# Feed-forward groups in another order, squares summed in parts, and the last shift shared between two engines

## The chip, the cores and the metric

The kernel runs on one core of one Trainium2 chip. The metric is the device time of one execution in microseconds (us). Five engines work side by side and wait for each other by semaphores: TensorE (PE, with its weight load PEld), VectorE (DVE), ScalarE (ACT), GpSimd (POOL) and SyncE (SP, which here only issues transfers). Sixteen DMA engines move data between the chip's memory (HBM) and the on-chip memory (SBUF); TensorE writes its products to PSUM.

## The reference, cut to what matters

Two decoder layers are run for a prompt of 256 tokens and a sample group of 8 sequences of 4 tokens (288 tokens together), with model width 1024. Layer 0 mixes tokens by retention, layer 1 by gated DeltaNet (GDN); each is followed by a gated feed-forward of width 2816. Ahead of each of these four parts, and once more at the end, the activations are normed and modulated by vectors that are computed from a condition (adaLN):

```python
def ada_rmsnorm(x, g, shift, scale):
    xf = x.astype(jnp.float32)
    xn = xf * lax.rsqrt(jnp.mean(xf * xf, axis=-1, keepdims=True) + EPS) * g.astype(jnp.float32)
    return (xn * (1.0 + scale[:, None, :]) + shift[:, None, :]).astype(x.dtype)

def conv_ffn(h, buf, w_up, w_dw, b_dw, w_down):
    up = jnp.einsum('btd,df->btf', h, w_up)
    gate_br, val = up[..., :D_FF], up[..., D_FF:]
    conv, new_buf = causal_dwconv(gate_br, buf, w_dw)
    act = jax.nn.silu(conv + b_dw.astype(conv.dtype)) * val
    return jnp.einsum('btf,fd->btd', act, w_down), new_buf
...
        h = ada_rmsnorm(x, p['norm_ffn'][l], sh2, sc2)
        out, buf = conv_ffn(h, s_fconv[l], p['w_ffn_up'][l], p['w_ffn_dw'][l], p['b_ffn_dw'][l], p['w_ffn_down'][l])
        x = (x.astype(jnp.float32) + g2[:, None, :] * out.astype(jnp.float32)).astype(x.dtype)
    y = ada_rmsnorm(x, p['norm_final'], shf, scf)
```

The outputs are y, the new states of both mixers and the last rows of the convolutions.

## The kernel before

Activations lie transposed: x is 8 tiles of 128 channels by 288 tokens. Weights come from HBM in blocks of 128 x 1024 (512 KB). Each block is split into a high and a low part (`whi` by ACT, line 414; `wlo` by DVE, line 415), and each product is made of three: high by high, high by low, low by high (`product`, line 533). One block serves 24 matmuls of 288 columns.

**Feed-forward** (`ffn`). The 22 tiles of the inner width are worked in groups of four, four, four, four, four and two. For each tile there is a gate product `fg` and a value product `fv`, with convolution, silu and product on ACT and DVE between them, and the result is split into `fah` and `fal`. The down product of a group (`down`) runs after the up products of the next group. `down` walks over the 8 tiles of x: a group of four tiles gives 12 matmuls for each tile of x, a group of two gives 6. After them DVE adds the gated result to x (line 698), forms the sample part `dt` (line 700), and POOL adds that (line 702). In the last group ACT also squares the new tile of x (line 595, `sq`, the first one into `ssum`) and DVE adds it to `ssum` (line 599).

**The norm** (`token_rsqrt`, `modulated`). The squares are summed over channels by products with a column of ones (`st`, line 558, 3 products of one column for each part that is summed, one for each of three stretches of 128 tokens; each is two instructions in the profile). DVE works out the reciprocal root from the 3 columns (lines 545 to 550, eleven small instructions), TensorE spreads it over the partitions (`rb`, line 564), and DVE and ACT make the modulated tiles `hh` and `hl` (lines 621 to 634). In the last feed-forward (gate 11) the squares of tiles 5, 6 and 7 are not added by DVE but kept as parts of their own, so that `st_y` is 12 products; the other places have one part and 3 products.

**The condition's products** (`adaP`, line 453) are cut into steps and put in where TensorE would wait: before `st`, between `st` and `rb`, and behind it.

**The end** (`finish`). After the last norm the result `yt` goes out in four transfers of two tiles each, from SP and ACT in turn.

Loads are issued by SP in the order of a plan (`plan_weights`) as their buffers come free. The order of the instructions on each engine is set by the framework's scheduler from the recorded program; it is read below from the built program.

Of the kernel before, what the change touches and what calls it, by code (L numbers as in the profile page):

```python
# [14 lines left out]
P = 128  # L15
# [7 lines left out]
KH, VH = 8, 16  # L23
FF = 2816
FT = FF // P
HALF_TOK = (0, 128, T - 128)
RSQRT_MAGIC = 0x5F3759DF
QUANTUM = 6
# [34 lines left out]
SAMPLE_STEPS = 3  # L63
OUT_STEPS = 1
SQ_ADD = 5
QK_STEPS = 5
ROOT_STEPS = 4
V_STEPS = 2
# [108 lines left out]
def blocks_out(w):  # L177

    out = []
    k0 = 0  # L180
    while k0 < w.shape[0]:
        n = min(4, (w.shape[0] - k0) // P)
        c = 1024 // n
        g = w[k0 : k0 + n * P].reshape(n, P, DM)
        for q in range(DM // c):
            out.append(g[:, :, q * c : (q + 1) * c].transpose(1, 0, 2).reshape(P, n * c))
        k0 += n * P
    return np.stack(out)
# [105 lines left out]
class Program:  # L294
# [12 lines left out]
    def plan_weights(self):  # L307
        A = self.A
        ada = lambda ch: [("ada", ch, k, A["wada"][ch * KT + k]) for k in range(KT)]
        wl = lambda name, i0, n: [("w", name, 0, A[name][i]) for i in range(i0, i0 + n)]  # L310

        def mix(main, extra, first=2):
            step = (len(main) - first - 1) * GROUP / max(1, len(extra))
            out, e = [], 0
            for i, m in enumerate(main):
                out.append(m)
                while e * GROUP < len(extra) and i >= first + e * step:
                    out += extra[e * GROUP : (e + 1) * GROUP]
                    e += 1
            return out + extra[e * GROUP :]  # L320


        second, step = ada(1), -(-KT // (EARLY - LATE))
        plan = [ada(0)]
        for i in range(EARLY):
            plan[0] += wl("wri", i, 1) + second[i * step : (i + 1) * step]
        ret = []
        for h in range(RH):
            ret += wl("wri", 12 * h, 12)
            if h:  # L330
                ret += wl("wro", 4 * (h - 1), 4)
        ret += wl("wro", 12, 4)
        fill = [sum((ada(ch) for ch in range(*r)), []) for r in FILL]
        plan.append(mix(ret[EARLY:], ada(2) + ada(3) + ada(4)) + fill[0])
        for l in range(2):
            f = []
            for g in range(6):
                f += wl(f"wu{l}", 8 * g, 8 if g < 5 else 4)
                if g:
                    f += wl(f"wd{l}", 4 * (g - 1), 4)  # L340
            f += wl(f"wd{l}", 20, 2)
            early = sum((ada(ch) for ch in ((range(FILL[0][1], FILL[1][0]), range(FILL[2][1], 14))[l])), [])
            plan.append(mix(f, early) + (fill[1] if l == 0 else []))
            if l == 0:
                f = wl("wba", 0, 1)
                first = {"K": 0, "V": 4, "Z": 8}
                chunk, more = F1, []
                for c, g in GDN_ORDER:
                    if c == "A":
                        more = ada(chunk)  # L350
                        chunk += 1
                        continue
                    w = wl("wgo", 4 * g, 4) if c == "D" else wl("wgi", 12 * g + first[c], 4)
                    for i, b in enumerate(w):
                        f += more[2 * i : 2 * i + 2] + [b]
                    more = []
                plan.append(f + fill[2])
        self.plan = [(*b, ph) for ph, part in enumerate(plan) for b in part]

        order, n = [], 0  # L360
        for ph, part in enumerate(plan):
            idx = list(range(n, n + len(part)))
            n += len(part)
            head = idx[:AHEAD] if ph > 1 else []
            order = order[: len(order) - (len(fill[ph - 2]) - AHEAD_AT if head else 0)] + head + (order[len(order) - (len(fill[ph - 2]) - AHEAD_AT) :] if head else []) + idx[len(head) :]
        self.order = order
        self.to_prep = [i for i, b in enumerate(self.plan) if b[0] == "w"]
        self.n_dma = self.n_prep = self.n_use = 0
        self.raw, self.split = {}, {}
        self.extra, self.held = {}, {"raw": 0}  # L370
        self.ada_todo = [i for i, b in enumerate(self.plan) if b[0] == "ada"]
# [180 lines left out]
    def token_rsqrt(self, ssum, scale, name):  # L552

        nc = self.nc
        st = self.aux(f"st_{name}")
        for i, t0 in enumerate(HALF_TOK):
            for n, s in enumerate(ssum):
                nc.tensor.matmul(st[:, i : i + 1], lhsT=s[:, t0 : t0 + P], rhs=self.ones[:, 0:1], start=(n == 0), stop=(n == len(ssum) - 1))
        r = self.tmp.tile([P, 3], F32, tag="tr", name=f"tr_{name}", bufs=2)
        self.rsqrt(r, st[:, 0:3], scale, EPS, name)  # L560
        yield from self.pause(ROOT_STEPS)
        rb = self.aux(f"rb_{name}")
        for i, c in enumerate((0, 0, P - TS)):
            nc.tensor.matmul(
                rb[:, i * P : i * P + P - c], lhsT=r[:, i : i + 1].to_broadcast([P, P]), rhs=self.ident[:, c:], start=True, stop=True
            )
        return rb[:, 0:T]
# [33 lines left out]
    def modulated(self, norm, sh, sc, name, hi, lo=None, rb=None, m0=0, m1=KT):  # L601

        nc = self.nc
        n, ms = m1 - m0, slice(m0, m1)
        am = self.tmp.tile([P, KT, 9], F32, tag="am", name=f"am_{name}", bufs=2)[:, 0:n]
        nb = self.prm("norms")[:, norm * KT + m0 : norm * KT + m1].unsqueeze(2).to_broadcast([P, n, 9])
        nc.vector.scalar_tensor_tensor(am, self.mod[:, sc * 8 + m0 : sc * 8 + m1, :], 1.0, nb, ALU.add, ALU.mult)
        shift = self.mod[:, sh * 8 + m0 : sh * 8 + m1, :]
        if rb is None:
            self.ada_due(FILLS[0])  # L610
            gen = self.token_rsqrt(self.ssum, 1.0 / DM, name)
            next(gen)

        hs = self.tmp.tile([P, T], F32, tag="t288", name=f"hs_{name}", bufs=T288)[:, : n * TS].rearrange("p (m t) -> p m t", m=n)
        by_t = lambda v: v.rearrange("p m (t b) -> p m t b", b=NB)
        by_b = lambda v: v[:, :, 1:9].unsqueeze(2).to_broadcast([P, n, TD, NB])
        nc.vector.tensor_tensor(by_t(hs), by_t(self.x[:, ms, TP:]), by_b(am), ALU.mult)
        if rb is None:
            self.ada_due(FILLS[1])
            rb = self.now(gen)  # L620
        nc.vector.tensor_tensor(hs, hs, rb[:, TP:].unsqueeze(1).to_broadcast([P, n, TS]), ALU.mult)
        if lo is None:
            nc.vector.tensor_tensor(by_t(hi[:, ms, TP:]), by_t(hs), by_b(shift), ALU.add)
        else:
            nc.vector.tensor_tensor(by_t(hs), by_t(hs), by_b(shift), ALU.add)
            nc.scalar.copy(hi[:, ms, TP:], hs)  # L626
            nc.gpsimd.tensor_tensor(lo[:, ms, TP:], hs, hi[:, ms, TP:].bitcast(F32), ALU.subtract)
        for i in range(n):
            m = m0 + i
            h = self.tmp.tile([P, T], F32, tag="t288", name=f"h_{name}", bufs=T288)[:, :TP]  # L630
            nc.vector.scalar_tensor_tensor(h, self.x[:, m, :TP], am[:, i, 0:1], rb[:, :TP], ALU.mult, ALU.mult)
            nc.scalar.activation(hi[:, m, :TP], h, AF.Identity, bias=shift[:, i, 0:1])  # L632
            if lo is not None:
                nc.vector.scalar_tensor_tensor(lo[:, m, :TP], h, shift[:, i, 0:1], hi[:, m, :TP].bitcast(F32), ALU.add, ALU.subtract)
        self.ada_due(FILLS[2])
# [50 lines left out]
    def down(self, wn, acts, kts, gate, last):  # L686
# [3 lines left out]
        for q in range(8 // per):  # L690
            w = self.weights(wn)
            for j in range(per):
# [8 lines left out]
                xv = xm[:, TP:].rearrange("p (t b) -> p t b", b=NB)  # L701
                (nc.vector if gate == 11 and last and m == KT - 1 else nc.gpsimd).tensor_tensor(xv, xv, t, ALU.add)  # L702
                if last:
                    self.squares(m, gate == 11)

    def stacked(self, out, src, which, mk):

# [200 lines left out]
    def ffn(self, l, hs, gate, after):  # L908
        nc, A = self.nc, self.A
        with ExitStack() as ctx:  # L910
# [8 lines left out]
            tail = fp.tile([P, FT, 2], F32, tag="tail", name="ftail")  # L919
            wd, bd = self.prm(f"wfd{l}"), self.prm(f"bfd{l}")  # L920
            pend = None
            for g in range(6):
                n = 4 if g < 5 else 2
                ah = ap.tile([P, 4, T], F32R, tag="ah", name=f"fah{l}{g}")
                al = ap.tile([P, 4, T], F32R, tag="al", name=f"fal{l}{g}")
                for j in range(n):
                    m = 4 * g + j
                    w = [wd[:, i * FT + m : i * FT + m + 1] for i in range(3)]
                    b = bd[:, m : m + 1]
                    pg = self.proj(hs, f"fg{l}{m}", f"wu{l}")  # L930
# [768 lines left out]
    def finish(self):  # L1699
        nc = self.nc  # L1700
        yt = self.hp.tile([P, KT, T], F32, tag="hh", name="yt")
        self.modulated(4, 12, 13, "y", yt)
        for c in range(0, KT, 2):
            (nc.sync, nc.scalar)[c // 2 % 2].dma_start(self.A["y"][:, c : c + 2], yt[:, c : c + 2])

# [22 lines left out]
```

## Time and profile before

| | |
|---|---|
| median of 3 runs | 1231.98 us (1230.52 to 1234.35) |
| profiled execution | 1235.09 us, of which the span of the profile is 1233.3 us |
| PE busy, PEld busy | 1162.4 us (94%), 1045.2 us (85%) |
| DVE, ACT, POOL busy | 877.2 us (71%), 608.4 us (49%), 326.0 us (26%) |
| chain that ended last | PE 77%, DVE 13%, ACT 3%, DMA 3%, issue 2% |
| HBM | 236.06 MB read, 31.39 MB written, 217 GB/s over the span |

The stages, in us from the span's start: start and retention to 343, the change to feed-forward 0 from 343 to 362, feed-forward 0 to 572, the change to GDN to 592, GDN to 973, the change to feed-forward 1 to 992, feed-forward 1 to 1215.5, the last norm and the output to 1233.3. "Granted clock" is the share of TensorE's full speed that it was given: 1.00 is 2.4 GHz and 0.50 is 1.2 GHz. A wait is named after the instruction that ended it.

### The profile page before, as it was taken

Reading aid. Unit: us, or ns where it says so; the run is one execution under the profiler, and the core shown is the slowest. Engines: PE = TensorE matmul, PEld = TensorE weight load, DVE = VectorE, ACT = ScalarE, POOL = GpSimd, SP = SyncE. Lnnn points to the kernel's source line nnn. Section 1 sums busy time; section 2 is a strip of 40 time slices with the busy share of each in tenths; the row PEclk is TensorE's granted clock in tenths of the full one; section 3 lists DMA queues with packets and bytes.
Section 4 is the critical chain, followed back from the end, with each engine's and each line's share of the span. In section 5 each row is a group of like instructions: output and inputs, shape, how many; then the busy total and the mean of one; then the engine's idle time right before and its main releaser. Section 6 shows DMA issues by size and latency. Waiting matters only on the chain.

```text
span 1233.3 us, 24974 instructions
## 1 busy us (share of the span) xinstructions
PE 1162.4 (94%) x9486; PEld 1045.2 (85%) x9486; DVE 877.2 (71%) x2038; ACT 608.4 (49%) x1258; POOL 326.0 (26%) x504
## 2 busy tenths in 40 slices
PE   6999999999999999999889888988899899999996
PEld 2879788797969999997777777977789699999996
DVE  3657574765766666667769888797965687878785
ACT  2444534344446445543674655745544365555542
POOL 0214142151301221233242124243222212233241
PEclk9999999999999999999989998999999899999997
DMA  9999696866689556556636652534334997878521
GB/s 350 347 335 331 224 338 230 315 239 236 226 298 400 196 161 199 171 181 243 219 84 209 218 165 61 161 129 120 126 109 130 307 358 257 258 238 264 182 76 39
DMA packets 97480, 269.08 MB, mean 218 GB/s; under 512 B 26816, under 2 KB 28832, under 8 KB 97232
## 3 DMA queue, kind: packets, MB, share of 16 engines
q1 hardware_dynamic: 87456, 234.42, 56.6%
q0 software_dynamic: 8032, 29.16, 6.3%
q10 hardware_dynamic: 1872, 3.90, 0.9%
q8 instruction: 75, 1.23, 0.4%
q14 instruction: 45, 0.37, 0.1%
HBM read 236.06 MB, written 31.39 MB: 217 GB/s over the span
## 4 chain that ended last, share of the span: by engine, by line
PE 77%; DVE 13%; ACT 3%; DMA 3%; issue 2%; POOL 1%; ACTq 0%; POOLq 0%; DVEq 0%
PE down L533 17%; PE fg L533 12%; PE fv L533 11%; PE pg L533 4%; PE pv L533 4%; PE adaP L453 4%; PE p L533 3%; PE gv L533 2%; PE gz L533 2%; DVE mp L1319 2%; DVE wlo L415 2%; PE gk L533 2%; PE pO L884 1%; PE pU L903 1%; PE pS L854 1%
## 5 line engine op out<-in xcount | busy, mean ns | idle before, releaser
L415 DVE TENSOR_TENSOR wlo<-more,whi 128x1024 fp32r<-128x1024 f32 x138 | 171.1, 1241 | 80.6 <-ACT whi L414 67.8
L414 ACT CAST whi<-more 128x1024 fp32r<-128x1024 f32 x138 | 144.4, 1048 | 139.6 <-PE down L533 53.3
L414 ACT CAST whi<-raw 128x1024 fp32r<-128x1024 f32 x123 | 128.0, 1044 | 146.3 <-PE down L533 44.1
L415 DVE TENSOR_TENSOR wlo<-raw,whi 128x1024 fp32r<-128x1024 f32 x123 | 154.2, 1256 | 60.6 <-ACT whi L414 36.5
L702 POOL TENSOR_TENSOR x<-x,dt 128x32 f32<-128x32 f32 x159 | 103.1, 649 | 138.9 <-DVE dt L700 137.2
L698 DVE SCALAR_TENSOR_TENSOR x<-down,mod,x 128x256 f32<-128x256 f32 x160 | 76.7, 479 | 52.5 <-PE down L533 51.9
L580 POOL TENSOR_TENSOR fal<-cv,fah 128x288 fp32r<-128x288 f32 x44 | 41.2, 936 | 217.3 <-ACT fah L579 186.3
L533 PE MATMUL down<-fal,whi 128*128 128x288 f32 x352 | 64.5, 295 | 0.0
L533 PE MATMUL down<-fah,whi 128*128 128x288 f32 x352 | 62.2, 294 | 0.0
L533 PE MATMUL down<-fah,wlo 128*128 128x288 f32 x352 | 62.1, 294 | 0.0
L904 DVE SCALAR_TENSOR_TENSOR S<-S,pU 128x512 f32<-128x512 f32 x64 | 42.2, 684 | 24.5 <-PE pU L903 24.4
L533 PE MATMUL fg<-hh_ffn,whi 128*128 128x288 f32 x352 | 58.4, 298 | 0.8 <-ACT hh_ffn L626 0.7
L533 PE MATMUL fv<-hh_ffn,whi 128*128 128x288 f32 x352 | 58.7, 297 | 0.0
L533 PE MATMUL fg<-hh_ffn,wlo 128*128 128x288 f32 x352 | 55.0, 296 | 0.0
L533 PE MATMUL fv<-hh_ffn,wlo 128*128 128x288 f32 x352 | 54.7, 295 | 0.0
L533 PE MATMUL fv<-hl_ffn,whi 128*128 128x288 f32 x352 | 54.2, 295 | 0.0
L533 PEld LDWEIGHTS fg<-hh_ffn,whi 128*128 128x128 f32 x352 | 50.3, 188 | 4.6 <-ACT hh_ffn L632 2.2
L533 PE MATMUL fg<-hl_ffn,whi 128*128 128x288 f32 x352 | 54.0, 295 | 0.0
L533 PEld LDWEIGHTS down<-fal,whi 128*128 128x128 f32 x352 | 52.4, 188 | 0.4 <-issue 0.4
L533 PEld LDWEIGHTS down<-fah,whi 128*128 128x128 f32 x352 | 51.9, 188 | 0.8 <-ACT whi L414 0.8
L533 PEld LDWEIGHTS fv<-hh_ffn,whi 128*128 128x128 f32 x352 | 50.3, 188 | 2.5 <-ACT ftail L934 1.2
L533 PEld LDWEIGHTS down<-fah,wlo 128*128 128x128 f32 x352 | 51.9, 188 | 0.0
(467 smaller groups left out, 2921.3 us busy)
## 6 DMA issues: line engine op xcount, KB each, us to landing
more<-in_wu SPq DMA_DIRECT2D x73, 512.0 KB, 5.2
raw<-in_wada SPq DMA_DIRECT2D x69, 512.0 KB, 4.8
raw<-in_wgi SPq DMA_DIRECT2D x48, 512.0 KB, 3.9
more<-in_wada SPq DMA_DIRECT2D x43, 512.0 KB, 6.3
more<-in_wd SPq DMA_DIRECT2D x36, 512.0 KB, 3.8
S<-in_sr SPq DMA_DIRECT2D x16, 1024.0 KB, 8.5
out_rs<-S POOLq DMA_DIRECT2D x16, 1024.0 KB, 6.9
raw<-in_wri SPq DMA_DIRECT2D x28, 512.0 KB, 4.6
```

Source lines behind the costliest of these rows:

```text
L414: nc.scalar.copy(hi[:, :c], r)
L415: nc.vector.tensor_tensor(lo[:, :c], r, hi[:, :c].bitcast(F32), ALU.subtract)
L453: nc.tensor.matmul(self.adaP[32 * g : 32 * g + 32, 0:256], lhsT=self.cs[:, k, :], rhs=rv[:, :, g, :], start=(k == 0), stop=(k == KT - 1), ...
L533: self.nc.tensor.matmul(out, lhsT=av[:, k, c0 : c0 + m], rhs=b[:, k, :], start=(k0 == 0 and i == 0), stop=(k1 == kts and i == len(seq) - 1))
L580: (nc.gpsimd if pool_lo else nc.vector).tensor_tensor(lo, src, hi.bitcast(F32), ALU.subtract)
L698: nc.vector.scalar_tensor_tensor(xm[:, :TP], p[:, :TP], g[:, 0:1], xm[:, :TP], ALU.mult, ALU.add)
L702: (nc.vector if gate == 11 and last and m == KT - 1 else nc.gpsimd).tensor_tensor(xv, xv, t, ALU.add)
L854: nc.tensor.matmul(pS, lhsT=kt[:, j, c * P : (c + 1) * P], rhs=vt[:, j, :], start=(j == 0), stop=(j == 1))
L884: nc.tensor.matmul(pO4[32 * g : 32 * g + 32, :], lhsT=qm[:, c, 4 * bb + g, :], rhs=S[bb, c][:, g, :], start=(bb == 0 and c == 0), stop=Fal ...
L903: nc.tensor.matmul(pU, lhsT=kms[g][:, c * P : (c + 1) * P], rhs=vst, start=True, stop=True)
L904: nc.vector.scalar_tensor_tensor(S[bb, c][:, g, :], S[bb, c][:, g, :], gamma4, pU, ALU.mult, ALU.add)
L1319: nc.vector.tensor_tensor(m, Ti[:, 0:k, :].rearrange("p j c -> p c j").unsqueeze(1).to_broadcast([P, w, 8, k]), X[:, 0:k, i:k].rearrange(" ...
```

## The change

1. The feed-forward's groups become two, four, four, four, four, four. The plan of loads and the layout of the down weights follow: the block pair of the two tiles comes first. The count of blocks, products and bytes is the same.
2. `squares` is called in its "end" form at all four places: three additions by DVE (tiles 5, 6 and 7) go at the end of retention, of feed-forward 0 and of GDN, and each of these norms has four parts, 12 products instead of 3. `token_rsqrt` walks over the parts outside and over the token stretches inside, so that only the last 3 products need the last tile's square.
3. In the last norm, the sample part's shift is added by POOL instead of DVE, and the prompt part of tile 2 by POOL instead of ACT.
4. The four output transfers carry tiles 0 to 3, 4 and 5, 6, and 7.

```diff
+FF_GROUPS = [(0, 2)] + [(2 + 4 * g, 4) for g in range(5)]
+POOL_TILE = 2
@@ blocks_out
-        n = min(4, (w.shape[0] - k0) // P)
+        n = 2 if (w.shape[0] - k0) // P % 4 else 4
@@ plan_weights
-            for g in range(6):
-                f += wl(f"wu{l}", 8 * g, 8 if g < 5 else 4)
+            for g, (m0, n) in enumerate(FF_GROUPS):
+                f += wl(f"wu{l}", 2 * m0, 2 * n)
                 if g:
-                    f += wl(f"wd{l}", 4 * (g - 1), 4)
-            f += wl(f"wd{l}", 20, 2)
+                    f += wl(f"wd{l}", *((0, 2) if g == 1 else (4 * g - 6, 4)))
+            f += wl(f"wd{l}", 18, 4)
@@ token_rsqrt
-        for i, t0 in enumerate(HALF_TOK):
-            for n, s in enumerate(ssum):
-                nc.tensor.matmul(st[:, i : i + 1], lhsT=s[:, t0 : t0 + P], rhs=self.ones[:, 0:1], start=(n == 0), stop=(n == len(ssum) - 1))
+        for n, s in enumerate(ssum):
+            for i, t0 in enumerate(HALF_TOK):
+                nc.tensor.matmul(
+                    st[:, i : i + 1], lhsT=s[:, t0 : t0 + P], rhs=self.ones[:, 0:1],
+                    start=(n == 0 and i == 0), stop=(n == len(ssum) - 1 and i == 2), skip_group_check=True,
+                )
@@ modulated
         if lo is None:
-            nc.vector.tensor_tensor(by_t(hi[:, ms, TP:]), by_t(hs), by_b(shift), ALU.add)
+            nc.gpsimd.tensor_tensor(by_t(hi[:, ms, TP:]), by_t(hs), by_b(shift), ALU.add)
...
-            nc.scalar.activation(hi[:, m, :TP], h, AF.Identity, bias=shift[:, i, 0:1])
+            if lo is None and i == POOL_TILE:
+                nc.gpsimd.tensor_scalar(hi[:, m, :TP], h, shift[:, i, 0:1], None, ALU.add)
+            else:
+                nc.scalar.activation(hi[:, m, :TP], h, AF.Identity, bias=shift[:, i, 0:1])
@@ down
-                    self.squares(m, gate == 11)
+                    self.squares(m, True)
@@ ffn
-            for g in range(6):
-                n = 4 if g < 5 else 2
+            for g, (m0, n) in enumerate(FF_GROUPS):
...
-                    m = 4 * g + j
+                    m = m0 + j
@@ finish
-        for c in range(0, KT, 2):
-            (nc.sync, nc.scalar)[c // 2 % 2].dma_start(self.A["y"][:, c : c + 2], yt[:, c : c + 2])
+        for i, (c, d) in enumerate(((0, 4), (4, 6), (6, 7), (7, 8))):
+            (nc.sync, nc.scalar)[i % 2].dma_start(self.A["y"][:, c:d], yt[:, c:d])
```

The order on TensorE between retention's last down product and feed-forward 0, before (`adaP` are products for the condition, `st_ffn` the sums of squares, `rb_ffn` the spread root):

```order
L453 MATMUL adaP<-raw,c 32x256 x5
L558 MATMUL st_ffn_3804<-ones,ssum 128x1 x3
L453 MATMUL adaP<-raw,c 32x256 x11
L462 MATMUL adaT<-cst,adaev 128x128 x2
L453 MATMUL adaP<-more_3786,c 32x256 x4
L564 MATMUL rb_ffn_3865<-cst,tr_ffn_3808 128x128 x2
```

and now:

```order
L455 MATMUL adaP<-raw,c 32x256 x4
L561 MATMUL st_ffn_3801<-ones,ssum 128x1 x3
L561 MATMUL st_ffn_3801<-ones,sq 128x1 x9
L455 MATMUL adaP<-raw,c 32x256 x12
L464 MATMUL adaT<-cst,adaev 128x128 x2
L455 MATMUL adaP<-more_3783,c 32x256 x4
L570 MATMUL rb_ffn_3871<-cst,tr_ffn_3814 128x128 x2
```

All twelve sums stand behind 14 instead of 15 products for the condition (the last row of these is shown), and one more product stands between them and `rb`.

The order on TensorE between feed-forward 0 and GDN, before (names as above; 32 products of `adaP` in seven rows stand ahead, the last three are shown):

```order
L453 MATMUL adaP<-more_6230,c 32x256 x4
L453 MATMUL adaP<-more_6232,c 32x256 x4
L453 MATMUL adaP<-more_6234,c 32x256 x4
L558 MATMUL st_gdn<-ones,ssum 128x1 x3
L462 MATMUL adaT<-cst,adaev 128x128 x2
L453 MATMUL adaP<-more_6274,c 32x256 x4
L453 MATMUL adaP<-more_6308,c 32x256 x4
L453 MATMUL adaP<-more_6348,c 32x256 x4
L453 MATMUL adaP<-more_6388,c 32x256
L564 MATMUL rb_gdn<-cst,tr_gdn 128x128 x2
```

and now, where the first row is the last of 20 products:

```order
L455 MATMUL adaP<-more_6248,c 32x256 x4
L561 MATMUL st_gdn<-ones,ssum 128x1 x3
L561 MATMUL st_gdn<-ones,sq 128x1 x9
L455 MATMUL adaP<-more_6250,c 32x256 x4
L455 MATMUL adaP<-more_6252,c 32x256 x4
L455 MATMUL adaP<-more_6254,c 32x256 x4
L464 MATMUL adaT<-cst,adaev 128x128 x2
L455 MATMUL adaP<-more_6294,c 32x256 x4
L455 MATMUL adaP<-more_6334,c 32x256 x4
L455 MATMUL adaP<-more_6374,c 32x256 x4
L570 MATMUL rb_gdn<-cst,tr_gdn 128x128 x2
```

The sums moved ahead of 12 products, which with the transposition `adaT` now stand between them and `rb`: 24 products there instead of 13.

The order on TensorE at the end, before:

```order
L533 MATMUL down<-fah_14525,wlo 128x288 x2
L558 MATMUL st_y<-ones,ssum 128x1
L558 MATMUL st_y<-ones,sq 128x1 x3
L558 MATMUL st_y<-ones,ssum 128x1
L558 MATMUL st_y<-ones,sq 128x1 x3
L558 MATMUL st_y<-ones,ssum 128x1
L558 MATMUL st_y<-ones,sq 128x1 x3
L564 MATMUL rb_y<-cst,tr_y 128x128 x2
```

and now:

```order
L535 MATMUL down<-fal_14290,whi 128x288 x4
L535 MATMUL down<-fah_14289,wlo 128x288 x4
L561 MATMUL st_y<-ones,ssum 128x1 x3
L561 MATMUL st_y<-ones,sq 128x1 x9
L570 MATMUL rb_y<-cst,tr_y 128x128 x2
L570 MATMUL rb_y<-cst,tr_y 128x32
```

Before, the first three of the four products of each stretch could run ahead of the last square only in the first stretch; now nine of the twelve stand ahead of the three that read it. The last down products are of a group of four.

## Rows read from the trace of the kernel before

**Rows 1.** Windows, TensorE: us, PE busy (instructions), granted clock, DMA share, GB/s.
```profile
343.00:362.00 19.00, 16.76 (x169) 1.00 0.92 344
...
973.00:992.00 19.00, 15.54 (x142) 0.82 0.95 351
...
992.00:1197.00 205.00, 205.00 (x1645) 1.00 0.70 231
...
1197.00:1215.50 18.50, 18.48 (x141) 1.00 0.12 35
```

**Rows 2.** Timeline, retention to feed-forward 0: start, us, instructions, count [idle before <-releaser].
```profile
343.80 0.94 ACT L595 ACTIVATE sq<-x 128x288 f32<-128x288 f32 x2 [1.06 <-POOL x L702]
...
344.12 0.81 PE L453 MATMUL adaP<-raw,c 128*32 128x256 f32 x8
...
345.49 0.83 PE L558 MATMUL st_ffn<-ones,ssum 128*128 128x1 f32 x6 [0.56 <-DVE ssum L599]
...
346.25 1.50 PE L453 MATMUL adaP<-raw,c 128*32 128x256 f32 x22
...
349.22 0.86 PE L564 MATMUL rb_ffn<-cst,tr_ffn 128*128 128x128 f32 x6
```

**Rows 3.** Timeline, feed-forward 0 to gated DeltaNet, TensorE.
```profile
573.34 2.34 PE L453 MATMUL adaP<-more,c 128*32 128x256 f32 x40
...
576.72 0.83 PE L558 MATMUL st_gdn<-ones,ssum 128*128 128x1 f32 x6 [1.04 <-DVE ssum L599]
...
577.75 1.92 PE L453 MATMUL adaP<-more,c 128*32 128x256 f32 x26
...
579.87 0.82 PE L564 MATMUL rb_gdn<-cst,tr_gdn 128*128 128x128 f32 x6 [0.20 <-DVE tr_gdn L550]
```

**Rows 4.** Timeline, gated DeltaNet to feed-forward 1, TensorE.
```profile
975.95 0.83 PE L558 MATMUL st_ffn<-ones,ssum 128*128 128x1 f32 x6 [0.92 <-DVE ssum L599]
...
980.42 1.08 PE L453 MATMUL adaP<-raw,c 128*32 128x256 f32 x8 [0.24 <-DMA raw<-in_wada]
...
982.53 1.33 PE L564 MATMUL rb_ffn<-cst,tr_ffn 128*128 128x128 f32 x6
```

**Rows 5.** Windows, TensorE, around the two falls of the granted clock.
```profile
978.00:979.00 1.00, 0.00 (x0) 0.74 0.69 234
...
985.00:986.00 1.00, 1.00 (x19) 0.85 0.81 303
...
1217.00:1218.00 1.00, 0.90 (x5) 0.70 0.00 0
...
1220.00:1221.00 1.00, 1.00 (x6) 0.50 0.00 0
```

**Rows 6.** Chain of waits, the end: start us, us, engine, tile, line.
```profile
1216.54 0.90 ACT sq L595 x2
...
1217.48 4.01 PE st_y L558 x18
...
1223.70 1.50 PE rb_y L564 x6
```

**Rows 7.** Timeline of the output, and one window (five engines, clock, DMA share, GB/s).
```profile
1225.95 0.42 DVE L623 TENSOR_TENSOR yt<-hs_y,mod 128x256 f32<-128x256 f32 x1
...
1226.29 2.82 DVE L631 SCALAR_TENSOR_TENSOR h_y<-x,am_y,rb_y 128x256 f32<-128x256 f32 x7
...
1229.87 0.35 ACTq L1704 DMA_DIRECT2D out_y<-yt  x1
...
1231.00:1231.50 0.50, 0.00 (x0) 0.00 (x0) 0.00 (x0) 0.00 (x0) 0.00 (x0) 0.50 1.00 378
```

**Rows 8.** Groups by line: count | busy us, mean ns | idle before, releasers.
```profile
L698 DVE SCALAR_TENSOR_TENSOR x<-down,mod,x 128x256 f32<-128x256 f32 x160 | 76.7, 479 | 52.5 <-PE down L533 51.9
...
L1544 DVE SCALAR_TENSOR_TENSOR uS<-uS,egl,psS 128x128 f32<-128x128 f32 x128 | 35.8, 341 | 8.4 <-PE psS L1540 8.4
...
L627 POOL TENSOR_TENSOR hl_ffn<-hs_ffn,hh_ffn 128x256 fp32r<-128x256 f32 x2 | 1.6, 801 | 18.3 <-ACT hh_ffn L626 18.3
```

## The prediction

> **What bounds the kernel.** I read the windows of TensorE by stage first, then the chain of waits and the timeline at the four places where a norm stands, then the groups by line. In feed-forward 1 TensorE is busy in 205.00 of 205 us, and in its last group of two tiles still in 18.48 of 18.5 us [rows 1]: at 141 products in 18.5 us, 48 down products of a group of two cost 6.3 us of TensorE, the same as 48 anywhere else, and nothing of the heavier work on DVE and ACT beside them shows as a wait. So the reader is to see that the order of the groups is free for TensorE, and that what the change is worth is decided at the four norms: there TensorE waits for squares, sums and the root, busy in 16.76 of 19 us ahead of feed-forward 0 and in 15.54 of 19 us ahead of feed-forward 1 [rows 1].
>
> **The groups.** Same blocks, products, bytes: 0 us. What remains is the lag of the last update of x behind the last down product, and it is counted at each norm below. Against it: the group of two now runs in the middle, where in feed-forward 1 the updates of GDN's states share DVE. 8 updates of x at 479 ns must pass in 6.3 us, and each state step adds four instructions of 341 ns, 1.4 us [rows 8]. The scheduler put one such step there. Bounds: 0, since four PSUM tiles let TensorE run ahead, to 2.7 us if two steps lie bare. I take 0, as the trace has the same group at full TensorE rate with the additions of squares on DVE in the place of that step.
>
> **The norm ahead of feed-forward 0.** Before, the products for the condition end at 344.93 (344.12 + 0.81), the last square is ready at 344.74, the sums wait for DVE's addition and start at 345.49, and the next product follows at 346.25: 0.76 us for 3 sums, six instructions of 0.127 us [rows 2]. Now one condition product fewer stands ahead, so the sums start at about 344.85; all squares are there. Twelve sums are 24 x 0.127 = 3.05 us, to 347.9. That is 1.65 us later than 346.25, and one product more lies behind them. `rb` stands behind 16 products on the same engine and moves with them. The removed additions and the removed wait (0.56 us) are in this sum already. Bounds: -0.6 us, if only the last three sums lay bare, to +3.9 us with all 24 at 0.223 us (below). I take +1.7, as the sums run back to back.
>
> **The norm ahead of GDN.** Before, 64 instructions for the condition end at 575.68; 40 of them take 2.34 us, 0.0585 each. The sums start at 576.72 after a wait of 1.04 us, and `rb` starts at 579.87 after a wait for the root of only 0.20 us [rows 3]. Now 24 of these instructions stand behind the sums. The sums start at 575.68 - 1.4 = 574.3, which the earlier squares of a group of four allow (the last of 8 tiles has 12 products, 1.6 us, in which DVE clears the one before), and end at 577.3. Then come 1.4 us of products, ACT's copy with the transposition (1.0 us: in [rows 2], 1.47 us lie between the end of the 22 instructions at 347.75 and `rb` at 349.22, 8 of 0.0585 among them), and another 1.4 us: `rb` at 581.1, 1.2 us later, bound by TensorE and no more by the root. The chain goes on from `rb` through DVE, so this stays. Bounds: -0.2 (if the root decided) to +2.6 (sums at 0.223). I take +1.2.
>
> **The norm ahead of feed-forward 1.** The sums end later by up to 2 us (before, 975.95 + 0.76; now 24 x 0.127 from 975.03, where the wait of 0.92 us began, so 978.1), but `rb` at 982.53 stands behind products that wait for a weight block until 980.42 [rows 4]. The root takes about 2.1 us and is there at 980.3. So 0 us. Bounds: +0.5, if the block is called for later, to -1.1, if the engine no longer loses its clock there (a rival below).
>
> **The last norm.** The last two squares end at 1217.44, and 18 of the 24 instructions of the sums come after them, 4.01 us at 0.223 each, to 1221.5 [rows 6]. Now the sums start with the end of the down products at 1215.5, 18 instructions need no late square, and the last tile's square is ready by about 1216.9 (0.48 us for x [rows 8], and about 0.9 for the sample part and the square, half of the 0.90 that two take [rows 6] in it). With 0.127 us each until the clock falls (1217.4, as before) and 0.223 behind, 15 + 9 instructions end at 1215.5 + 1.9 + 2.0 = 1219.4: -2.1 us; at 0.127 throughout, 1218.5: -3.0 us. I take -2.5.
>
> **The output.** DVE loses 0.42 us (0.34 of the path, as its instructions overlap), but the bytes decide: after the last transfer is issued at 1229.87, the engines still move 378 GB/s in 1231.0 to 1231.5 [rows 7]. 1.18 MB (288 tokens x 1024 x 4 bytes) at that rate are 3.1 us, so the end is set by when the first transfer starts. Now it waits for four tiles instead of two: two more at 2.82 / 7 = 0.40 us, less 0.34 us, and for POOL's two instructions (nearest row 0.80 us for 128 x 256 beside DVE [rows 8]), which end about with ACT's tile 3. I take +0.2; bounds -0.4 (smaller last piece) to +0.8 (POOL at 1.2 us for each).
>
> **The clock.** TensorE's granted clock goes from 1.00 to 0.50 at about 978.5 and 1217.4 (0.74 and 0.70 in those windows) [rows 5]. After the second fall it stays at 0.50 although TensorE is busy without a gap in 1220 to 1221 [rows 5], all through the 4.01 us of one-column sums [rows 6]; it came back at 985.3, behind wide products [rows 5]. So one-column sums do not bring the clock back, and 3 us of them now stand in three places in which there were 0.8 us. If the clock falls there, the 22 instructions behind cost 22/8 x 1.08 = 2.9 us instead of 1.50 [rows 2, 4]: +1.4. I expect this at one of the two places ahead of feed-forward 0 and GDN with even chance: +0.7.
> The Trainium skill (TensorE: Matmul & The Clock Gate, Part 1: The HAM clock gate) says that the clock depends on how busy TensorE has been of late. By that, sums without a gap would keep it up, and the sum would be without this term, 1232.6 us. The trace has the engine busy without a gap at half the clock, so I side with the row. This is the first rival below.
>
> **Sum.** 0 + 1.7 + 1.2 + 0 - 2.5 + 0.2 + 0.7 = +1.3 us. The profiled execution took 1235.09 us (span 1233.3 us and 1.8 us around it) and would take 1236.4; it is 3.1 us above the median of the runs shown, 1231.98, from which I count: 1233.3 us. A change is told from none here by 0.3%, 3.7 us.
>
> **Rivals.**
> 1. The clock stays up at all places, at the norm ahead of feed-forward 1 too, where it falls before. For it: that fall came in a stretch in which TensorE idled, and the sums now fill some of it. Against it: rows 5, as told. Then `rb`, 1.33 us at half clock against 0.86, and the products ahead of it come earlier by 1.1 us, and the last norm gains 3.0: 1.7 + 1.2 - 1.1 - 3.0 + 0.2 = -1.0, 1231.0 us. With less than I count at the first two norms it would go to -3.7 and beyond.
> 2. Slower: the clock falls at the norms ahead of feed-forward 0 and of GDN, both, and comes back only with the dense products. Place: from the sums to `rb` and behind it. Price: ahead of feed-forward 0, 32 condition instructions (+2.0) and `rb` (+0.5); ahead of GDN, 48 instructions (+3.1) and `rb` (+0.5). 1.7 + 2.5 + 1.2 + 3.6 - 2.1 + 0.2 = +7.1, 1239.1 us. It decides from the point where more than half of this is paid. For it: rows 5. Against it: the stretch of sums is shorter than the one at the end, and wide products stand on both sides.
> 3. The group of two in the middle of feed-forward 1 makes DVE the bound, +2 in place of 0 (bounds above): 1235.3 us. Against it: the full TensorE rate in [rows 1].
>
> **Chances.** The forecast 0.50 (its own range 1231.4 to 1235.4), rival 1 0.24, rival 2 0.17, rival 3 0.09. Faster by over 3.7 us: a third of rival 1 and a little of the forecast, 0.12. Slower by over 3.7 us: most of rival 2 and a third of rival 3, 0.17. Within: 0.71. The range for 8 in 10 is 1229.2 to 1237.2: below it lies the outer part of rival 1, above it half of rival 2.
>
> **What would show it.** Right: 24 instructions of sums ahead of feed-forward 0 in about 3.05 us and `rb` there 1.6 us or more later behind the last down product; `rb` ahead of GDN bound by TensorE; `rb` ahead of feed-forward 1 still behind the awaited block; the last sums ending 3.0 to 3.9 us behind the last down product instead of 6.0; TensorE at 205 of 205 us in feed-forward 1; about 8.3 us from `rb`'s end to the span's end. Wrong: sums that overlap other products, a TensorE wait for PSUM or for DVE in the first down products of feed-forward 1, or an output that ends with the issue of its last piece and not with the bytes.

## The result, and the profile after

The changed kernel takes 1242.61 us (median of 9 runs, 1236.99 to 1246.96), the kernel before 1232.23 us beside it: ratio 1.0073 [1.0054, 1.0093], which is 9 us slower (the two medians lie 10.4 us apart). In two later series, each on one chip with runs of before beside it, the ratio was 1.0029 [1.0013, 1.0045] and 1.0046 [1.0023, 1.0069]: slower each time, by 3.6 to 9 us. The forecast, 1233.3 us (1229.2 to 1237.2), was too low, and its likeliest verdict, no difference, was wrong. The profiled execution took 1238.67 us (span 1235.9), 4 us under its own median, so its trace shows the smaller form of the loss.

Windows of TensorE after (columns as in [rows 1]): the change to feed-forward 0, the change to feed-forward 1, and feed-forward 1 in the two stretches that answer to the last rows there.

```profile
343.00:362.00 19.00, 17.24 (x162) 0.91 0.85 291
978.50:997.50 19.00, 16.92 (x147) 0.82 0.91 344
997.50:1202.50 205.00, 205.00 (x1641) 1.00 0.69 230
1202.50:1221.00 18.50, 18.50 (x143) 1.00 0.08 30
```

The feed-forward itself is as full as before (205.00 of 205 us). The first row is where it differs from [rows 1]: busier, but at a granted clock of 0.91 instead of 1.00. The second row is busier too, at the same mean clock, but its window is not the same stretch of work: it begins 1.0 us behind the last down product, the one of before 0.6 us ahead of it.

The timeline of TensorE from the last down product of retention to `rb` (columns as in [rows 2], which answers to it), and the clock in four windows of it.

```profile
345.03 0.80 PE L455 MATMUL adaP<-raw,c 128*32 128x256 f32 x6
345.76 0.83 PE L561 MATMUL st_ffn<-ones,ssum 128*128 128x1 f32 x6
346.45 2.15 PE L561 MATMUL st_ffn<-ones,sq 128*128 128x1 f32 x18
348.53 2.58 PE L455 MATMUL adaP<-raw,c 128*32 128x256 f32 x24
...
352.83 0.85 PE L570 MATMUL rb_ffn<-cst,tr_ffn 128*128 128x128 f32 x6
```

```profile
348.00:349.00 1.00, 1.00 (x14) 0.90 0.99 381
349.00:350.00 1.00, 1.00 (x12) 0.50 1.02 393
350.00:351.00 1.00, 1.00 (x12) 0.50 1.02 418
351.00:352.00 1.00, 0.47 (x6) 0.50 1.31 315
```

The 24 sum instructions run back to back at full clock in 2.84 us, and just behind them the clock goes to 0.50 while TensorE is still 1.00 busy. The 24 instructions for the condition take 2.58 us; at full clock they take 1.50. The same place between feed-forward 0 and GDN, against [rows 3]:

```profile
578.39 0.83 PE L561 MATMUL st_gdn<-ones,ssum 128*128 128x1 f32 x6
579.09 2.33 PE L561 MATMUL st_gdn<-ones,sq 128*128 128x1 f32 x18
581.35 2.79 PE L455 MATMUL adaP<-more,c 128*32 128x256 f32 x24
...
585.05 1.50 PE L455 MATMUL adaP<-more,c 128*32 128x256 f32 x24
586.48 0.85 PE L570 MATMUL rb_gdn<-cst,tr_gdn 128*128 128x128 f32 x6
```

Here the fall comes inside the sums, and 24 condition instructions take 2.79 us; the next 24, at full clock again, take 1.50. The norm ahead of feed-forward 1 has a fall of the clock before as after ([rows 4, 5]):

```profile
984.49 1.08 PE L455 MATMUL adaP<-raw,c 128*32 128x256 f32 x8 [0.58 <-DMA raw<-in_wada]
986.12 0.69 PE L464 MATMUL adaT<-cst,adaev 128*128 128x128 f32 x2 [0.55 <-ACT adaev L461]
986.59 1.33 PE L570 MATMUL rb_ffn<-cst,tr_ffn 128*128 128x128 f32 x6
```

The end, from the chain of waits (columns as in [rows 6]); below it the output in the timeline, and three windows, one in the sums and two in the output (five engines, clock, DMA share, GB/s), against [rows 7].

```profile
1202.37 18.25 PE down L535 x138
1220.62 3.00 PE st_y L561 x24
...
1225.82 1.50 PE rb_y L570 x6
```

```profile
1227.85 0.70 POOL L629 TENSOR_TENSOR yt<-hs_y,mod 128x256 f32<-128x256 f32 x1 [7.86 <-DVE hs_y L627]
...
1229.05 0.93 POOL L639 TENSOR_SCALAR yt<-h_y,mod 128x256 f32<-128x256 f32 x1 [0.50 <-DVE h_y L637]
...
1230.00 1.44 SPq L1712 DMA_DIRECT2D out_y<-yt  x2
...
1231.97 0.35 ACTq L1712 DMA_DIRECT2D out_y<-yt  x1
```

```profile
1222.00:1223.00 1.00, 1.00 (x9) 1.00 (x9) 0.00 (x0) 0.00 (x0) 0.00 (x0) 0.80 0.00 0
...
1233.00:1233.50 0.50, 0.00 (x0) 0.00 (x0) 0.00 (x0) 0.00 (x0) 0.00 (x0) 0.50 0.97 320
...
1234.00:1234.50 0.50, 0.00 (x0) 0.00 (x0) 0.00 (x0) 0.00 (x0) 0.00 (x0) 0.50 0.08 25
```

All 24 sum instructions of the last norm end 3.0 us behind the last down product (6.0 before). The output ends with the bytes, as said, 8.6 us behind `rb` (8.1 before).

One measure for all kernels, the names being those of the next section, worked out from the timelines of one execution each: us from the end of the last down product to the first up product (`fg` in a feed-forward, `gk` in GDN), in brackets the us at 0.50 of the falls between 342 and 366, 572 and 606, 970 and 1006 (in `sums_repeat` and `repeat_wide` the same places, which stand 9 to 21 us later); for the last norm, to the start of `rb`.

| kernel | to feed-forward 0 | to GDN | to feed-forward 1 | last norm |
|---|---|---|---|---|
| before | 8.7 (0) | 11.0 (0) | 12.3 (6.8) | 8.2 |
| after | 11.4 (3.4) | 13.7 (3.4) | 13.1 (6.8) | 5.2 |
| after_again | 11.5 (3.4) | 12.2 (0) | 12.5 (6.8) | 4.8 |
| after_third | 10.1 (0) | 16.7 (10.2) | 12.3 (6.8) | 4.8 |
| one_part_norms | 8.7 (0) | 10.2 (0) | 13.0 (6.8) | 4.8 |
| one_part_again | 8.7 (0) | 10.2 (3.4, behind `gk`) | 12.4 (6.8) | 4.8 |
| groups_alone | 8.7 (0) | 10.2 (3.4, behind `gk`) | 12.7 (6.8) | 5.8 |
| tail_alone | 9.5 (0) | 11.0 (0) | 11.7 (6.8) | 6.0 |
| two_parts | 8.8 (0) | 10.9 (0) | 13.4 (6.8) | 5.2 |
| parts_alone | 11.8 (10.2) | 17.3 (13.7, 3.4 of it behind `gk`) | 13.1 (10.2) | 5.3 |
| repeat_three | 12.0 (3.4) | 14.4 (6.8, 3.4 of it behind `gk`) | 13.1 (6.8) | 7.5 |
| sums_repeat | 14.0 (13.7) | 14.4 (3.4) | 13.3 (10.2) | 6.9 |
| repeat_wide | 12.1 (0) | 13.1 (3.4, behind `gk`) | 10.6 (0) | 6.5 |
| sums_spread | 11.0 (0) | 13.1 (0) | 14.3 (10.2) | 5.0 |
| wide_norms | 12.3 (0) | 12.3 (3.4, behind `gk`) | 10.5 (0) | 4.8 |
| wide_sums | 11.7 (0) | 12.3 (3.4, behind `gk`) | 11.3 (0) | 4.9 |
| one_part_wide | 10.2 (0) | 10.3 (0) | 13.7 (6.8) | 4.9 |

### The profile page after: what moved, and what is told of

It reads as the page before. It is cut to its first block, busy times and chain, and to the rows that moved or that the text cites. A ratio compares the mean times of both kernels' runs of the same rounds, so it can differ in the third digit from the quotient of the medians.

```text
span 1235.9 us, 25069 instructions
## 1 busy us (share of the span) xinstructions
PE 1170.4 (95%) x9540; PEld 1053.1 (85%) x9540; DVE 873.0 (71%) x2028; ACT 608.6 (49%) x1257; POOL 323.6 (26%) x506
## 4 chain that ended last, share of the span: by engine, by line
PE 78%; DVE 12%; DMA 4%; ACT 3%; issue 2%; POOL 1%; SPq 0%; ACTq 0%; DVEq 0%; POOLq 0%
PE down L535 18%; PE fg L535 12%; PE fv L535 11%; PE pg L535 4%; PE adaP L455 4%; PE pv L535 4%; PE p L535 3%; PE gv L535 3%; DVE mp L1327 2%; PE gz L535 2%; PE gk L535 2%; DVE wlo L417 1%; PE pO L893 1%; PE pU L912 1%; DVE Ti L1331 1%
## 5 line engine op out<-in xcount | busy, mean ns | idle before, releaser
L711 POOL TENSOR_TENSOR x<-x,dt 128x32 f32<-128x32 f32 x159 | 100.0, 631 | 136.6 <-DVE dt L709 134.8
L535 PEld LDWEIGHTS fg<-hh_ffn,whi 128*128 128x128 f32 x352 | 50.4, 189 | 5.6 <-ACT hh_ffn L641 2.6
```

Of the source, the lines that this page charges most:

```text
L535: self.nc.tensor.matmul(out, lhsT=av[:, k, c0 : c0 + m], rhs=b[:, k, :], start=(k0 == 0 and i == 0), stop=(k1 == kts and i == len(seq) - 1))
```

## The experiments

**Which part.** Four kernels, each with one part undone or alone.

```diff
one_part_norms (from after):
-                    self.squares(m, True)
+                    self.squares(m, gate == 11)
parts_alone (from before): squares(m, True) and the loop over parts outside, nothing else
groups_alone (from before): FF_GROUPS in ffn, plan_weights, blocks_out, nothing else
tail_alone (from before): the loop over parts, POOL's two shifts, the output's pieces
```

> The changed kernel with one part undone: DVE adds all squares at the three inner norms again, so st_ffn, st_gdn and st_ffn are 3 products each; groups, last norm and output as changed. Theory A (the 12 one-column sums at three norms, and the half clock that follows them, are the loss): 1230 to 1233 us, that is 9 to 12 us below the changed kernel's 1242.6 and at or a little below before's 1232.2; the granted clock stays 1.00 in the windows ahead of feed-forward 0 and of GDN. Theory B (the order of the groups and the plan of loads is the loss): still 1238 to 1243 us. Theory C (POOL's share and the output's pieces): still 1238 to 1243 us, with the excess behind rb_y.

Measured: 1230.92 us, ratio to before 0.9984 [0.9968, 0.9999].

> The kernel before with one part of the change alone: four parts at every norm and the loop over parts outside (12 one-column sums at the three inner norms). Theory A: 1238 to 1242 us, the clock at 0.50 for some us behind the sums ahead of feed-forward 0 and of GDN, rb there 2.5 us later or more. Theory B and C: 1230 to 1233 us.

Measured: 1241.29 us, 1.0066 [1.0047, 1.0085].

> The kernel before with the group of two first, alone (plan and layout of the down weights with it). Theory A: within 2 us of before, 1231 to 1234 us, TensorE 100% busy in both feed-forwards. Theory B: 1238 to 1242 us. Theory C: as before.

Measured: 1231.05 us, 0.9986 [0.9970, 1.0003].

> The kernel before with the end of the change alone: the loop over parts outside (it touches the last norm only, the others have one part), POOL's two shifts, the output in pieces of 4, 2, 1 and 1 tiles. Theory A: 1229.5 to 1232 us (last sums -2 us, output +0.2). Theory B: the same. Theory C: 1238 us or more, with the excess behind rb_y.

Measured: 1232.27 us, 0.9993 [0.9978, 1.0009], a little above its range.

Theory A holds and B and C fall: the parts at the three inner norms alone make the loss, and without them the change is a small gain. In the trace of `parts_alone` the clock stays down for 10.2 us at each of the three inner norms, against 3.4 to 6.8 us in the first trace of after. TensorE is busy without a gap, with the condition's products, and still at 0.50 (windows behind its sums ahead of GDN):

```profile
584.00:585.00 1.00, 1.00 (x10) 0.50 1.00 410
588.00:589.00 1.00, 1.00 (x10) 0.50 0.90 287
591.00:592.00 1.00, 1.00 (x6) 0.50 0.82 336
```

**Products or clock.** The parts bring 18 more instructions to each norm and a fall of the clock. Four kernels were meant to tell the two apart.

```diff
wide_sums (from after, all norms and retention's heads):
-                    st[:, i : i + 1], lhsT=s[:, t0 : t0 + P], rhs=self.ones[:, 0:1],
+                    st[:, i * P : (i + 1) * P], lhsT=s[:, t0 : t0 + P], rhs=self.ones[:, 0:P],
...  (DVE reads the first of each 128 columns)
sums_spread (from after, inner norms; ada_due(1) ahead of the first part):
         for n, s in enumerate(ssum):
+            if n and not last:
+                self.ada_due(2)
two_parts (from after, inner norms):
-        if m >= (SQ_ADD if end else KT):
+        if m >= (SQ_ADD if end else 7):
...  (and squares(m, gate == 11), as in one_part_norms)
one_part_wide: one_part_norms with the lines of wide_sums
```

> The changed kernel with each sum of squares made 128 columns wide instead of one (the right side is 128 equal columns of ones, DVE reads the first of each 128); order and count of instructions are the same. An instruction of rb, 128 columns wide, takes 0.143 us (six in 0.86), one of the one-column sums 0.116 (24 in 2.77), so a norm's sums take up to 0.6 us more. Theory A1 (the narrow products let the clock fall: it is not held by an engine that is busy but moves one column at a time): granted clock 1.00 in the windows ahead of feed-forward 0 and of GDN, the last sums at full clock, median 1232 to 1237 us against 1242.6. Theory A2 (the time of 18 more instructions at each norm and what stands behind them is the loss, the clock is a side effect): 1243 to 1245 us. Theory A3 (any products that read the squares, or the order of the work there, let the clock fall): 1242 to 1245 us with the clock at 0.50 as in the changed kernel.

Measured: 1235.29 us, 1.0018 [1.0000, 1.0036]. The order was not wholly the same, as it had been expected: ahead of feed-forward 0, 8 condition products (16 instructions) moved in front of `rb`. In its trace the clock held from the sums to the first up product at all three inner norms (table), as theory A1 had it.

> The changed kernel with the four parts' one-column sums set apart by 8 condition products each at the three inner norms (in feed-forward 0's norm by 6, 8 and 8), instead of 12 sums on end; nothing is added. Theory A1 with length (a long unbroken run of one-column sums costs the clock): the clock stays at 1.00 ahead of feed-forward 0 and of GDN, 1234 to 1238 us. Theory A1 without length (one-column sums do not count, wherever they stand among few wide products): it falls about as often, 1239 to 1243 us. Theory A2: the time of the sums stays, 1240 to 1243 us.

Measured: 1241.41 us, 1.0070 [1.0048, 1.0092], though in its trace the clock held ahead of feed-forward 0 and of GDN. No theory had that pair. The sums still lay on the path there (11.0 and 13.1 us in the table), the clock fell longer ahead of feed-forward 1, and GDN itself was 3 us longer than before's, with 34.1 us at 0.50 in that stage against 27.3. Over all its runs the mean granted clock gives 53.3 us at half clock, and 54.0 for the runs of before beside them (the measure is explained under "On one chip"). So in this order a loss as large came without more half clock than before: the clock is not the only way to it. The table has 2.3 and 2.1 us more than before ahead of feed-forward 0 and of GDN without a fall; the rest of its loss is not located.

> The changed kernel with two parts instead of four at the three inner norms (only tile 7 apart, 6 sums, 12 instructions; two more additions by DVE each). Theory A1: half the length, about 1.5 us of one-column sums at each norm; if the fall comes with length, most of the loss is gone: 1232 to 1236 us; if the loss is by instruction (A2), a third of it stays: 3 of 9 added sums, 1234 to 1237 us, with the clock at 1.00.

Measured: 1233.62 us, 0.9998 [0.9984, 1.0012]: half the sums, and no fall at either place. The loss is not in proportion to the instructions.

> The changed kernel with DVE's additions back at the three inner norms (one part, 3 sums) and all sums 128 columns wide: the candidate to beat both. Theory A1: the last norm's 24 instructions and rb stay at full clock, some 2 us less than with narrow sums there: 1227 to 1230 us against 1230.9 without the wide columns. Theory A2 and A3: 1231 to 1232 us.

Measured: 1230.95 us, 0.9990 [0.9977, 1.0004]: no gain from the width. What was to be won at the last norm was not there: with narrow sums too the clock held through its 24 instructions in the trace of `one_part_norms` (4.8 us in the table, 4.9 here).

**One-column sums without the parts.** Before's kernel makes its 3 sums four times over.

```diff
sums_repeat (from before); repeat_wide has rhs=self.ones[:, 0:P] in it
+        for r in range(4 if len(ssum) == 1 and name != "ret" else 1):
           for i, t0 in enumerate(HALF_TOK):
```

> The kernel before, with DVE's additions and one part kept, whose three inner norms make their 3 one-column sums four times over into the same columns (12 products, 24 instructions; the last 3 are the ones used). Two terms: the 18 more instructions at 0.12 us lie on the path ahead of feed-forward 0 and of GDN, 2.2 us each and nothing ahead of feed-forward 1 (4.4 us together); and the clock, 4 to 7 us. If both are right: 1240 to 1245 us with falls of the clock to 0.50 behind the sums. If the parts themselves (squares kept apart, DVE freed, sums started early) made the loss: 1236 to 1238 us, the products' time alone.

Measured: 1255.55 us, 1.0171 [1.0150, 1.0191].

> The same with all sums of these three norms 128 columns wide; the order is the same but for 8 condition products that stand ahead of rb instead of behind it in the norm of feed-forward 0 (16 instructions, 1.0 us). If the narrow columns cost the clock: the products' time alone remains, 1237 to 1239 us, no fall to 0.50 ahead of feed-forward 0 and of GDN. If the width is of no account: as sums_repeat plus 1 us.

Measured: 1243.35 us, 1.0082 [1.0053, 1.0110].

Both came out too slow because the edit also caught the four head norms inside retention, which have one part too: 4 x 18 instructions x 0.116 us = 8.4 us more, and in both the last down product of retention ends at 352 us instead of 343. The pair still tells: as many products, 12 us apart, intervals clear of each other, and only the narrow one loses its clock inside or behind the sums (table). The mean granted clock of all their runs gives 75.7 us at half clock for the narrow and 40.2 for the wide one. The wide one has 8 condition products more ahead of `rb`; they stand behind the place where the narrow one's clock falls.

> The changed kernel once more on the chip of the two above, for a second execution in the trace. Theory: 1240 to 1244 us; half clock behind the sums at the same two or three places, for 3 to 10 us each, longer than in the first trace (3.4 us each), since the median is 4 us above that execution. If the falls are as short as in the first trace and the time is 1242 all the same, the clock explains less than 3 us of the loss.

Measured: 1238.17 us, 1.0029 [1.0013, 1.0045]. Neither case: at GDN the clock did not fall at all. Sums and condition products of the changed kernel in this execution, and one window:

```profile
579.37 2.15 PE L561 MATMUL st_gdn<-ones,sq 128*128 128x1 f32 x18
581.45 1.50 PE L455 MATMUL adaP<-more,c 128*32 128x256 f32 x24
...
585.30 0.85 PE L570 MATMUL rb_gdn<-cst,tr_gdn 128*128 128x128 f32 x6
```

```profile
581.00:582.00 1.00, 1.00 (x17) 1.00 1.02 393
```

**On one chip.** The three kernels that the size depends on, side by side, and `repeat_three`, which is `sums_repeat` at the three inner norms alone (`name[:3] in ("ffn", "gdn")`); `wide_norms` is `wide_sums` at these alone.

> The changed kernel with one part at the three inner norms, once more, as the base for the two below on one chip: 1229 to 1232 us if before is at 1232 to 1233, ratio to before 0.998 to 1.000.

Measured: 1230.23 us, 0.9973 [0.9950, 0.9995].

> The changed kernel on the same chip. Its excess over one_part_again is the loss by the three norms: two terms, the time of the 18 more instructions on the path ahead of feed-forward 0 and of GDN (4 us, always paid) and the clock (paid by chance: 0 to 10 us at half clock at a norm). Together 5 to 12 us; with only the products' time it would be 4 us.

Measured: 1239.29 us, 1.0046 [1.0023, 1.0069].

> The changed kernel with the sums 128 columns wide at the three inner norms only (heads of retention and last norm as changed; 8 condition products more stand ahead of rb in feed-forward 0's norm, up to 1 us). If the narrow columns cost the clock: no fall behind the sums, and the excess over one_part_again is the products' time alone, 4 to 5 us, less up to 1 us for the norm of feed-forward 1, where before's clock falls too. If the clock is not the cause of the rest: the same time as after_third, or 1 us more.

Measured: 1234.35 us, 1.0022 [1.0001, 1.0044].

> The kernel before, whose three inner norms make their 3 one-column sums four times over into the same columns; nothing else moves (sums_repeat had done that in the four head norms of retention too). DVE's additions and the one part stay. If one-column products alone make the loss: 4.4 us of products' time and the clock, 1238 to 1245 us, falls to 0.50 behind the sums. If the parts make it: at most 1238 us and no falls ahead of feed-forward 0 and of GDN.

Measured: 1241.03 us, 1.0073 [1.0045, 1.0100]: one-column sums alone make the loss; the squares need not be kept apart.

After less one part: 9.1 us. Of it, after less wide is 4.9 us, put down to the clock, and wide less one part 4.1 us, put down to the products. The split is rough: the intervals of after and wide overlap, and it is not clean. The wide kernel also keeps its clock ahead of feed-forward 1 (10.5 us in the table), where every kernel without 24 wide sums loses it (11.7 us or more), and pays for 8 products more ahead of `rb` in feed-forward 0's norm (12.3 us against 10.1 in `after_third`, both without a fall); the two are about 2 us each and opposite. In `after_third` the fall at GDN lasts through `rb` (timeline and windows), in `wide_norms` there is none there:

```profile
578.30 2.53 PE L561 MATMUL st_gdn<-ones,sq 128*128 128x1 f32 x18
580.77 2.79 PE L455 MATMUL adaP<-more,c 128*32 128x256 f32 x24
...
584.72 2.79 PE L455 MATMUL adaP<-more,c 128*32 128x256 f32 x24
587.43 1.49 PE L570 MATMUL rb_gdn<-cst,tr_gdn 128*128 128x128 f32 x6
```

```profile
580.00:581.00 1.00, 1.00 (x9) 0.50 1.03 397
585.00:586.00 1.00, 1.00 (x13) 0.50 1.04 377
589.00:590.00 1.00, 1.00 (x12) 0.50 0.00 0
```

```profile
579.13 2.17 PE L562 MATMUL st_gdn<-ones,sq 128*128 128x128 f32 x18
581.23 1.50 PE L455 MATMUL adaP<-more,c 128*32 128x256 f32 x24
...
585.08 0.85 PE L571 MATMUL rb_gdn<-cst,tr_gdn 128*128 128x128 f32 x6
```

The mean granted clock of each timed run points the same way. The us at half clock, 2 x (1 - mean clock) x span, are on this chip 57.4 on average for after, 50.4 for one_part_norms and 44.2 for wide_norms (54.7 for before, whose last norm runs its sums at half clock). The 7.0 us between the first two lose 3.5 us, if TensorE is busy in them. Over all chips it is 58.8 in 29 runs of after and 49.2 in 24 of one_part_norms, 4.8 us by the same count. The first series of after, the slowest, has 66.1 us, the two later ones 53.7 and 57.4: much of what sets the three apart is the clock. So the clock's share is about 3.5 to 4.9 us by these measures, and the rest is put down to time on the path, of which the table shows 3.4 us without a fall: 1.4 ahead of feed-forward 0 (10.1 against 8.7) and 2.0 ahead of GDN (12.2 against 10.2). Some 0.4 to 0.8 us lie outside the span of the profile: on average a run of after takes 2.2 to 2.6 us more than its span, one of one_part_norms 1.8. Why, stays open.

`one_part_norms` has the lowest ratio, 0.9984 and 0.9973 of before, 9 to 11 us below after. It is not told from `groups_alone` (0.9986) and `one_part_wide` (0.9990).

## Why the prediction was wrong

- **The step that failed: "The clock", +0.7 us.** It counted one short fall, of 1.4 us, with even chance at one of two places. Measured, the clock's share is about 3.5 to 4.9 us. A fall came behind or inside the sums at both places, each in 2 of 3 executions of after, and when it came it lasted 3.4 to 10.2 us (ahead of GDN, 12.2 us without a fall became 13.7 and 16.7). The price stopped at the 22 instructions behind the sums; in `after_third` it went on over 48 of them, `rb` and beyond. (22/8 x 1.08 is 2.97, not 2.9 us; that slip is not what failed.)
- **Rival 2 named the mechanism**: the clock falls at both norms and comes back late, 1239.1 us. It got 0.17. The argument against it, wide products on both sides, failed: the condition's products behind the sums ran 10 us at 0.50 with TensorE busy. Its +7.1 us stand against +9.0, +3.6 and +5.7 measured. It has the mechanism, but its size is near by luck in part: only one of the three traces of after has the fall at both norms.
- **The norms ahead of feed-forward 0 and GDN, +1.7 and +1.2 us**, hold for executions without a fall: 10.1 - 8.7 = +1.4, and 12.2 - 11.0 = +1.2. The lone sums cost what was said; but undoing the parts gave 10.2 at GDN, less than before, as with the group of four DVE's last addition ends 2.0 us behind the last down product instead of 4.6 (timelines of one_part_norms and before). So the parts are dearer there (2.0) than the sum shows.
- **Ahead of feed-forward 1, 0 us**: 12.3 to 13.1 against 12.3; `rb` stands behind the awaited block as before. The first execution is 0.7 longer, beyond the bound of +0.5, but without the parts it was 12.4 and 13.0: no effect is told from that spread.
- **The last norm, -2.5 us**: -3.0 to -3.4. The clock fell at about 1222.6 (0.80 in the window from 1222), 2.0 us behind the last down product, as forecast; by then fewer than the 9 instructions counted were left, since the sums run at 0.116 us and wait for no square. In the other two traces of after the clock did not fall before the sums had ended.
- **The output, +0.2 us**: 8.6 - 8.1 = +0.5, inside its bounds. POOL took 0.70 and 0.93 us.
- **The groups, 0 us**: groups_alone is not told from no change, so rival 3 falls too. Rival 1, the clock up everywhere, is refuted for after; the clock stayed up at all three inner norms only in the kernels with 24 wide sums.
- **The comparison of two executions misled** by its total: 1235.9 - 1233.3 is +2.6 us, near the forecast's +1.3. From the first `gk` to GDN's last down product that execution of before took 390.5 us and that of after 387.6; one_part_norms took 388.3 with the same work. So 3 us that the change does not explain hid part of the loss; and that execution of before lay 3 us above its median, that of after 4 us below.

## What to carry to other kernels

Before replacing additions on DVE by many small products on TensorE, count not only their time but what the clock does behind them: ask the trace what one such run did to the granted clock, and price the fall to where the clock returned there, not to the next instruction. Where the products must stay, half as many (`two_parts`) were not told from before here, and wide ones cost less than narrow ones (1234.35 against 1239.29 us). And take stage lengths of several executions before a difference of 3 us in one stage is read as an effect.

## What was not expected of the hardware

- A sum product 128 columns wide takes hardly longer than one of one column: 24 instructions in 2.94 us (`wide_norms`) and 2.84 us (after).
- With one-column sums, 24 instructions without a break, the clock fell inside or behind them in 10 of 12 cases (six executions, ahead of feed-forward 0 and of GDN: after three times, parts_alone, repeat_three, sums_repeat); with 128 columns in none of 6 (wide_sums, wide_norms, repeat_wide), at the same busy share of 1.00. At the last norm 24 narrow sums do not always cost it: the clock held through them in `after_again` and `one_part_norms`. Why a fall comes or not in the same program, stays open.
- The same program at the same place fell to half clock for 0, 3.4 or 10.2 us in three executions; between the shortest and the longest lie 4.5 us of stage length (12.2 and 16.7).
